# A bidirectional encoder block on one core: two feature tiles side by side in the opening

## The chip, the cores and the metric

One core of one Trainium2 chip runs the whole program. The metric is the device time of one execution in microseconds (us), measured as the median of several runs; lower is better. The core has TensorE (matrix products, "PE" in the profile, with "PEld" for its weight loads), VectorE ("DVE"), ScalarE ("ACT"), GpSimd ("POOL"), and SyncE ("SP"), whose queue issues nearly all transfers here.

## The reference

Two groups of tokens, a prompt of 2048 and a sample of 512, go through one layer of a hybrid encoder with shared weights. Sixteen learned meta tokens stand ahead of each.

```python
u = rms_norm(h, norm_g)
proj = u @ w_in                      # 1024 -> 5376, cut into ten parts
qa, ka, va, za, qb, kb, vb, zb, ga, gb = jnp.split(proj, cuts, axis=-1)
o_a = neighbourhood_attention(qa, ka, va, na_rpb, n)     # branch A: 8 x 16 window on a 64-wide grid
o_b = window_attention(qb, kb, vb, t5_bias, sink, n)     # branch B: +-128 tokens, 8 query and 2 key heads
y_a = (o_a * jax.nn.silu(za)) @ w_proj_a
y_b = (o_b * jax.nn.silu(zb)) @ w_proj_b
merged = jax.nn.sigmoid(ga) * y_a + jax.nn.sigmoid(gb) * y_b
h = h + merged @ w_out
y = rms_norm(h[:, N_META:], final_g)                     # rms_norm: x * rsqrt(mean(x*x) + 1e-6) * g
```

All inputs and outputs are float32.

## The kernel before

Everything is kept feature-major: 128 features on the partitions, tokens along the free dimension. The 2560 tokens are five windows of 512 (window 0 is the sample, 1 to 4 the prompt). The 5376 output features of the input projection are 42 feature tiles of 128: branch A's queries are tiles 0 to 3 (`QA`), its keys 4 to 7 (`KA`), its values 8 to 11 (`VA`), its gate path from 12; branch B's queries are 16 to 19 (`QB`), then `KB`, `VB` and its gate path; the merge gates are 26 to 41.

Products are in float32 precision built of three: every operand is split into a rounded high part and the low remainder (`split`, `split_w`, `split_part`: a cast on ScalarE, then a subtraction on VectorE that needs the cast's result), and `mm3` (L143 to L146) adds high x high, high x low and low x high. One feature tile over 512 tokens is therefore 8 input tiles x 3 = 24 products of 128x512, and `project` yields after each quarter of them, that is after two input tiles or 6 products.

The program begins with the last window, which is done alone (`alone`, `beside`), while the inputs of windows 0 and 1 are prepared beside it; these two are then multiplied together in a scheme with fewer products (`begin`, `pairs`). The opening is made of these parts:

- `start_w(firsts)` fetches and splits the weights of the first feature tiles. Raw weights (`wraw`, 512 KB a tile) and split ones (`wt`) have two buffers each, so a third fetch waits for the first tile's split, and a third split for the end of the first tile's products.
- `prep_last(True)` loads the last window's x in four pairs of tiles (`xt`, 512 KB each) and the 16 meta columns (`xm`), scales them by the norm's gain (`ng`) into the high part (ScalarE, L325) and the low part (VectorE, L326), squares them in place (ScalarE, L328) and adds the squares (VectorE, L330, L333). Its later steps, each ended by a `yield`, form the column sums by products with ones (`fin_v`, L351, L352), take the inverse root (`rsqrt`), put it on a diagonal (`diagonal`, L175) and spread it over the partitions by products with ones (`spread`, L183), which are copied to `rs`. The scale is applied only when a product is stored, so products run ahead of the norm and the stores of the first tiles are held back (`held`) until it is there.
- `prep_first` loads windows 0 and 1 (`x`, eight transfers of 512 KB, in two halves), squares them (L409), adds the squares for one window on GpSimd and for the other on VectorE (L411, L414), then does the same norm and forms the operands.
- `zero_rows` writes zeros into twelve places of the value buffers in HBM; all transfers share the queue of SyncE in program order.
- `beside` goes through `firsts` (branch A's queries, branch B's queries, A's keys, A's values, `KB`, `VB`) tile by tile and counts quarters in `q`. At quarters 9 and 14 it takes the two later steps of `prep_last`, at quarters 2, 20, 27, 28 and so on those of `prep_first`. With tile i it fetches the weights of tile i + 3 and splits the next one's.

`store` puts a finished tile away: `put_q` scales it (L272), splits it (L244, L245) and writes it to HBM; a query tile of branch A is written twice over (1 MB), one of branch B once (512 KB).

TensorE's and SyncE's orders are those of the program (`manual_schedule`). On ScalarE, VectorE and GpSimd a planner sets the order, from its own timeline and the program order; `issue_after` adds an edge to it.

After the opening come the pairs of windows 0 and 1, the same for 2 and 3 (with `prep_ahead` beside the first), then attention and the dense layers window by window, and the last window's end.

Of the kernel before, what the change touches and what calls it, by code (L numbers as in the profile page):

```python
# [17 lines left out]
P = 128  # L18
# [77 lines left out]
def encoder_block(ctx: ExitStack, tc: tile.TileContext, xT, x_end, w_in, w_pa, w_pb, w_o, norm_g, final_g,  # L96
# [42 lines left out]
    def move(out, in_):  # L139
        last_move[0] = nc.sync.dma_start(*(f32(a) if a.dtype == F32R else a for a in (out, in_)))  # L140
        return last_move[0]
# [3 lines left out]
        nc.tensor.matmul(ps, wh, ul, start=False, stop=False)  # L145
        nc.tensor.matmul(ps, wl, uh, start=False, stop=last)  # L146

    def rsqrt(small, sq, m, nc_):

        ve, hv, r, t = (small.tile([P, 8], F32, tag=f"rs{i}", name=f"rs{i}")[:m, :nc_] for i in range(4))  # L150
        nc.vector.tensor_scalar(ve, sq, 1.0 / D_MODEL, EPS, ALU.mult, ALU.add)
        nc.vector.tensor_scalar(r.bitcast(I32), ve.bitcast(I32), 1, None, ALU.arith_shift_right)
        nc.vector.tensor_scalar(r.bitcast(I32), r.bitcast(I32), -1.0, float(0x5F3759DF), ALU.mult, ALU.add)
        nc.vector.tensor_scalar(hv, ve, -0.5, None, ALU.mult)
        for _ in range(3):
            if nc_ == 1:
                nc.vector.scalar_tensor_tensor(t, r, hv, r, ALU.mult, ALU.mult)
            else:
                nc.vector.tensor_mul(t, r, hv)
                nc.vector.tensor_mul(t, t, r)  # L160
            nc.vector.scalar_tensor_tensor(r, t, 1.5, r, ALU.add, ALU.mult)
        return r
# [34 lines left out]
    def split_part(h, l, r, eng=None):  # L197
        nc.scalar.copy(h, r)  # L198
        low[0] = (eng or lo_eng[0]).tensor_sub(l, r, f32(h)).ins  # L199
# [8 lines left out]
    class Weights:  # L208
# [50 lines left out]
    def finish(gen):  # L259
        r = None  # L260
        for r in gen:
            pass
        return r
# [41 lines left out]

        return (up if i < 5 else uxp).tile(shape, F32R, tag=f"u{i}", name=name)

    def prep_last(meta):


        w = NWIN - 1
        uh, ul = (operand(i, [P, KT, PITCH], f"u4{i}") for i in (5, 6))
        us[w] = (uh, ul, us[w][2] if w in us else uxp.tile([P, UW + N_META], F32, tag="rs4", name="rs4")[:, :UW])
        rs = us[w][2]
        for k in range(0, KT, 2):
            rows = xT[k * P : (k + 2) * P]
            xt = ev.tile([P, 2, WTOK], F32, tag="ev", name="xt")
            move(xt, rows[:, w * WTOK : (w + 1) * WTOK].rearrange("(k p) t -> p k t", p=P))
            if meta and k == 0:
                xm = st.tile([P, KT, N_META], F32, tag="xm", name="xm", bufs=1)  # L320
                move(xm, xT[:, TOK:].rearrange("(k p) t -> p k t", p=P))
            for j in range(2):
                g = ng[:, k + j : k + j + 1]
                h = uh[:, k + j, :WTOK]
                nc.scalar.mul(h, xt[:, j, :], g)  # L325
                nc.vector.scalar_tensor_tensor(ul[:, k + j, :WTOK], xt[:, j, :], g, f32(h), ALU.mult, ALU.subtract)  # L326
            if meta:
                nc.scalar.activation(xt, xt, AF.Square)  # L328
                if k == 0:
                    nc.vector.tensor_add(rs[:, :WTOK], xt[:, 0, :], xt[:, 1, :])  # L330
                else:
                    for j in range(2):
                        nc.vector.tensor_add(rs[:, :WTOK], rs[:, :WTOK], xt[:, j, :])  # L333
        if not meta:
            return
        t = ev.tile([P, WTOK], F32, tag="t", name="xms", bufs=3)
        a, b = (t[:, i * P : (i + 1) * P].rearrange("p (k m) -> p k m", m=N_META) for i in range(2))
        nc.vector.tensor_mul(a, xm, ng[:, :, None].broadcast_to([P, KT, N_META]))
        mh, ml = uh[:, :, WTOK:UW], ul[:, :, WTOK:UW]
        nc.scalar.copy(mh, a)  # L340
        nc.vector.tensor_sub(ml, a, f32(mh))
        nc.scalar.activation(b, xm, AF.Square)
        for n in (4, 2):
            nc.vector.tensor_add(b[:, :n], b[:, :n], b[:, n : 2 * n])
        nc.vector.tensor_add(rs[:, WTOK:], b[:, 0], b[:, 1])
        yield
        sq = st.tile([P, 32], F32, tag="sq", name="sq", bufs=1)[:, :5]
        nc.vector.memset(sq, 1.0)
        v = ps_t.tile([P, WTOK], F32, tag="vt", name="fin_v")
        for c in range(4):  # L350
            nc.tensor.matmul(v[:, c : c + 1], rs[:, c * P : (c + 1) * P], ones[:, 0:1], start=True, stop=True)  # L351
        nc.tensor.matmul(v[:N_META, 4:5], rs[:, WTOK:], ones[:, 0:1], start=True, stop=True)  # L352
        nc.scalar.copy(sq[:, :4], v[:, :4])
        nc.scalar.copy(sq[:N_META, 4:5], v[:N_META, 4:5])
        r = rsqrt(uxp, sq, P, 5)
        dgs = [ev.tile([P, WTOK], F32, tag="t", name="rs_dg", bufs=3) for _ in range(2)]
        diagonal(dgs[0], r[:, :4], P)
        diagonal(dgs[1], r[:N_META, 4:5], N_META)
        yield
        for dg, c0, m, nc_ in (dgs[0], 0, P, 4), (dgs[1], WTOK, N_META, 1):  # L360
            nc.scalar.copy(rs[:, c0 : c0 + nc_ * m], spread(ps_t, "vt", dg, m, nc_)[:, : nc_ * m])
        yield
# [25 lines left out]
    def prep_first(sp, wa, loaded):  # L388
# [28 lines left out]
        for i in range(2):  # L417
            for c in range(4):
                nc.tensor.matmul(v[:, 4 * i + c : 4 * i + c + 1], rss[i][:, c * P : (c + 1) * P], ones[:, 0:1],
                                 start=True, stop=True)  # L420
        r = rsqrt(uxp, v[:, :8], P, 8)
        dgs = [ev.tile([P, WTOK], F32, tag="t", name="rs_dg", bufs=3) for _ in range(2)]
        for i in range(2):
            diagonal(dgs[i], r[:, 4 * i : 4 * i + 4], P)
# [32 lines left out]
    def prep_ahead(w):  # L457
# [21 lines left out]
        r = rsqrt(uxp, v[:, :8], P, 8)  # L479
# [429 lines left out]
    def beside(fs, raws, wts, own, wa, steps, at):  # L909

        held = [own, None if own is None else []]
        ws = [*fs, *both[0]]
        lag[0] = 4
        mark[0] = None
        at = list(at)
        q = 0
        for i, f in enumerate(fs):
            if i:  # L920
                wts.append(split_w(raws[i + 1]))
                if i + 3 < len(ws):
                    raws.append(fetch_w(w_in[ws[i + 3]]))
            for _ in alone(f, wts[i], held):
                q += 1
                if own is not None and q in own[1]:
                    next(own[0])
                    if q == own[1][-1]:
                        for fn in held[1]:
                            fn()  # L930
                        held[1] = None
                while at and at[0] <= q:
                    at.pop(0)
                    next(steps)
# [13 lines left out]
    order = [*range(0, KA + 2), VA, VA + 1, KA + 2, KA + 3, QB, QB + 1, VA + 2, VA + 3, QB + 2, QB + 3, KB, VB,  # L948
             *range(ZA, QB), *range(ZB, 42)]
    both = list(zip(order[::2], order[1::2]))  # L950
    firsts = [*range(QA, KA), *range(QB, KB), *range(KA, ZA), KB, VB]
    rest = [f for f in range(GA) if f not in firsts]

    def start_w(fs):
        raws = [fetch_w(w_in[f]) for f in fs[:1]]
        wts = [split_w(raws[0])]
        yield raws, wts
        raws.append(fetch_w(w_in[fs[1]]))
        raws.append(fetch_w(w_in[fs[2]]))
        yield  # L960
        wts.append(split_w(raws[1]))
        raws.append(fetch_w(w_in[fs[3]]))
        yield
# [3 lines left out]
            pool = [pp.enter_context(tc.tile_pool(name=f"p{i}", bufs=1, reuse_waits="tile")) for i in range(3)]  # L967
            return pairs(pool, wa, wa + 1, both, a, first.send(pool[2]), raw1, ahead, extra, opening)

    w0 = start_w(firsts)  # L970
    raws, wts = next(w0)
    own = prep_last(True)
    next(own)
    with tc.tile_pool(name="sp", bufs=1, reuse_waits="tile") as sp:
        loaded = []
        steps = prep_first(sp, 0, loaded)
        next(w0)
        next(steps)
# [677 lines left out]
```

## Time and profile before

| | us |
|---|---|
| median of 3 runs | 1897.26 |
| lowest and highest | 1896.54, 1899.39 |
| the profiled execution | 1896.82 |
| its span, first to last instruction | 1894.7 |
| TensorE busy in it | 1863.0 |

A row of the timeline reads: start, duration, engine, source line, operation, tile written <- tiles read, shapes, count, and in brackets the idle time of the engine before it with what ended that. "SPq" rows are transfers being issued, not transferred. A row of the windows reads: stretch, its length, then busy time and count for TensorE, its weight loads, VectorE, ScalarE and GpSimd, the granted clock, the mean busy share of the DMA engines, and GB/s. In a row of the waits, the engine, tile and line on the left waited for what stands on the right: microseconds in total, times, longest.

### The profile page before, as it was taken

Reading aid. Unit: us, or ns where it says so; the run is one execution under the profiler, and the core shown is the slowest. Engines: PE = TensorE matmul, PEld = TensorE weight load, DVE = VectorE, ACT = ScalarE, POOL = GpSimd, SP = SyncE. Lnnn points to the kernel's source line nnn. Section 1 sums busy time; section 2 is a strip of 40 time slices with the busy share of each in tenths; the row PEclk is TensorE's granted clock in tenths of the full one; section 3 lists DMA queues with packets and bytes.
Section 4 is the critical chain, followed back from the end, with each engine's and each line's share of the span. In section 5 each row is a group of like instructions: output and inputs, shape, how many; then the busy total and the mean of one; then the engine's idle time right before and its main releaser. Section 6 shows DMA issues by size and latency. Waiting matters only on the chain. (4 is left out here: it accounts for less than half of the span.)

```text
span 1894.7 us, 29723 instructions
## 1 busy us (share of the span) xinstructions
PE 1863.0 (98%) x9797; PEld 1585.1 (84%) x9797; DVE 1341.5 (71%) x2939; ACT 1144.3 (60%) x2523; POOL 733.1 (39%) x556
## 2 busy tenths in 40 slices
PE   8999999999999999999999999999999999999998
PEld 6898888888888888888888888888888888888886
DVE  8886666556477565444457888878888887888874
ACT  6454444444365444444456787897788778778932
POOL 2005442323102232323224336656754864585420
PEclk9999999999999999999999999999999999999999
DMA  7667756644296787644268878967976996697483
GB/s 262 236 177 293 209 173 183 212 172 178 84 354 227 218 222 199 201 135 160 106 218 306 264 230 264 305 201 254 314 246 216 290 313 212 213 315 253 125 289 141
DMA packets 290385, 424.83 MB, mean 224 GB/s; under 512 B 117416, under 2 KB 162040, under 8 KB 288696
## 3 DMA queue, kind: packets, MB, share of 16 engines
q1 hardware_dynamic: 289944, 422.93, 69.2%
q8 instruction: 78, 1.28, 0.3%
q14 instruction: 75, 0.61, 0.1%
q10 hardware_dynamic: 288, 0.01, 0.0%
HBM read 303.46 MB, written 119.39 MB: 223 GB/s over the span
## 5 line engine op out<-in xcount | busy, mean ns | idle before, releaser
L199 POOL TENSOR_TENSOR wt<-wraw,wt 128x512 fp32r<-128x512 f32 x164 | 215.0, 1328 | 283.9 <-ACT wt L198 283.9
L826 PE MATMUL pa<-u,wt 128*128 128x512 f32 x1008 | 242.7, 390 | 0.0
L826 PE MATMUL pa<-u,x 128*128 128x512 f32 x984 | 236.8, 389 | 0.9 <-ACT u L837 0.9
L198 ACT CAST wt<-wraw 128x512 fp32r<-128x512 f32 x312 | 177.7, 619 | 77.0 <-PE mm L146 36.4
L826 PEld LDWEIGHTS pa<-u,wt 128*128 128x128 f32 x1008 | 188.8, 188 | 39.1
L826 PEld LDWEIGHTS pa<-u,x 128*128 128x128 f32 x984 | 184.4, 188 | 40.1 <-ACT u L837 1.7
L797 POOL TENSOR_TENSOR s<-wraw,raw 128x512 f32<-128x512 f32 x40 | 58.3, 1457 | 275.1 <-DVE x L199 275.1
L144 PE MATMUL mm<-u,wt 128*128 128x512 f32 (+2 forms) x416 | 150.8, 362 | 8.0 <-ACT u L325 7.4
L792 POOL TENSOR_TENSOR s<-raw 128x512 f32<-128x512 f32 x40 | 58.4, 1461 | 253.5 <-DMA raw<-in_w_in_dram 250.1
L146 PE MATMUL mm<-u,wt 128*128 128x512 f32 (+2 forms) x416 | 147.1, 354 | 1.9 <-DVE wt L199 1.9
L145 PE MATMUL mm<-u,wt 128*128 128x512 f32 (+2 forms) x416 | 147.0, 353 | 0.7 <-DVE u L326 0.7
L199 DVE TENSOR_TENSOR wt<-wraw,wt 128x512 fp32r<-128x512 f32 x148 | 107.9, 767 | 53.2 <-ACT wt L198 52.8
L826 PE MATMUL pe<-u,wt 128*128 128x512 f32 x504 | 121.3, 390 | 0.0
L826 PE MATMUL pc<-u,wt 128*128 128x512 f32 x504 | 121.1, 389 | 0.0
L826 PE MATMUL pe<-u,x 128*128 128x512 f32 x480 | 115.3, 389 | 0.0
L826 PEld LDWEIGHTS pc<-u,wt 128*128 128x128 f32 x504 | 94.6, 188 | 19.6
L826 PEld LDWEIGHTS pe<-u,wt 128*128 128x128 f32 x504 | 94.5, 188 | 19.6
L1122 DVE TENSOR_TENSOR pl<-tp,ph 128x384 fp32r<-128x384 f32 (+6 forms) x160 | 94.5, 591 | 22.3 <-ACT ph L1121 20.6
L144 PE MATMUL pso<-mh,wt 128*128 128x512 f32 x256 | 107.1, 418 | 0.0
L805 POOL TENSOR_TENSOR s<-wraw,s 128x512 f32<-128x512 f32 x40 | 55.0, 1374 | 131.5 <-DVE wt L199 131.5
L826 PEld LDWEIGHTS pe<-u,x 128*128 128x128 f32 x480 | 90.1, 188 | 18.7
L1027 ACT ACTIVATE prs<-s,nm 128x402 f32<-128x402 f32 (+1 forms) x160 | 91.0, 571 | 20.8 <-DVE nm L1020 17.7
(246 smaller groups left out, 5028.0 us busy)
## 6 DMA issues: line engine op xcount, KB each, us to landing
wraw<-in_w_in_dram SPq DMA_DIRECT2D x86, 512.0 KB
qa<-evq SPq DMA_DIRECT2D x20, 1024.0 KB
raw<-in_w_in_dram SPq DMA_DIRECT2D x40, 512.0 KB
q<-qa SPq DMA_DIRECT2D x20, 1024.0 KB
wraw<-in_w_o_dram SPq DMA_DIRECT2D x32, 512.0 KB
kbt<-kb SPq DMA_DIRECT2D x32, 384.0 KB
qb<-evq SPq DMA_DIRECT2D x20, 512.0 KB
ka<-evk SPq DMA_DIRECT2D x20, 512.0 KB
```

Of the source, the lines that this page charges most:

```text
L144: nc.tensor.matmul(ps, wh, uh, start=first, stop=False)
L145: nc.tensor.matmul(ps, wh, ul, start=False, stop=False)
L146: nc.tensor.matmul(ps, wl, uh, start=False, stop=last)
L198: nc.scalar.copy(h, r)
L199: low[0] = (eng or lo_eng[0]).tensor_sub(l, r, f32(h)).ins
L792: eng.tensor_add(s1, a21, a22)
L797: eng.tensor_sub(s3, a11, a21)
L805: eng.tensor_sub(s4, a12, s2)
L826: nc.tensor.matmul(ps, wt[:, a, s], u[:, b, kk, :], start=first and kk == 0 and i == 0, stop=kk == 3 and i == 2, skip_group_check=True)
L1027: nc.scalar.activation(out, s, AF.Exp, bias=nm, scale=-1.0, accum_out=sm)
L1122: nc.vector.tensor_sub(pl_[:kb, a], tb, f32(ph_[:kb, a]))
```

## The change

The opening is rewritten in these points.

1. The first two feature tiles are done side by side. `start_two` fetches their weights by halves (256 KB each) and splits each half by itself; `prep_last` takes it as a generator `between` and moves it on between the x loads and between the scalings, so that transfers are issued as: first tile's lower half, x tile 0, x tile 1, second tile's lower half, x tiles 2 and 3, both upper halves, the other x tiles. In `beside`, `first_two` alternates the quarters of the two tiles 0, 1, 0, 1, 0, 0, 1, 1.
2. The meta columns are loaded behind all x of the window.
3. Nine products of ones with ones, 128x128, go to TensorE ahead of everything. Nothing reads their result.
4. The squares of `prep_last` are placed behind all scalings, in a step of their own; `issue_after` holds them there on ScalarE.
5. `firsts` begins with branch B's queries, then branch A's.
6. The steps beside the tiles move: `prep_last`'s from quarters 9 and 14 to 10 and 15, `prep_first`'s second from 20 to 22.
7. In `rsqrt`, the half term is computed from the sums and not from the step before it, and in the input norms the root `r` lives in columns 8 to 15 of the accumulator bank that holds the sums (`place`); `prep_last`'s two copies of the sums are gone.

```diff
-    def rsqrt(small, sq, m, nc_):
+    def rsqrt(small, sq, m, nc_, place=None):
         ve, hv, r, t = (small.tile([P, 8], F32, tag=f"rs{i}", name=f"rs{i}")[:m, :nc_] for i in range(4))
+        if place is not None:
+            r = place[:m, :nc_]
...
-        nc.vector.tensor_scalar(hv, ve, -0.5, None, ALU.mult)
+        nc.vector.tensor_scalar(hv, sq, -0.5 / D_MODEL, -0.5 * EPS, ALU.mult, ALU.add)
...
-    def prep_last(meta):
+    def prep_last(meta, between=None):
...
+        xts = []
         for k in range(0, KT, 2):
             xt = ev.tile([P, 2, WTOK], F32, tag="ev", name="xt")
-            move(xt, rows[:, w * WTOK : (w + 1) * WTOK].rearrange("(k p) t -> p k t", p=P))
-            if meta and k == 0:
-                xm = st.tile([P, KT, N_META], F32, tag="xm", name="xm", bufs=1)
-                move(xm, xT[:, TOK:].rearrange("(k p) t -> p k t", p=P))
+            xts.append(xt)
+            for j, n in ((0, 1), (1, 1)) if meta and k == 0 else ((0, 2),):
+                move(xt[:, j : j + n], xT[(k + j) * P : (k + j + n) * P, w * WTOK : (w + 1) * WTOK]
+                     .rearrange("(k p) t -> p k t", p=P))
+            if between is not None:
+                next(between, None)
             for j in range(2):
...
-                nc.scalar.mul(h, xt[:, j, :], g)
+                scaled = nc.scalar.mul(h, xt[:, j, :], g)
                 nc.vector.scalar_tensor_tensor(ul[:, k + j, :WTOK], xt[:, j, :], g, f32(h), ALU.mult, ALU.subtract)
-            if meta:
-                nc.scalar.activation(xt, xt, AF.Square)
...
+            if between is not None:
+                next(between, None)
         if not meta:
             return
+        xm = st.tile([P, KT, N_META], F32, tag="xm", name="xm", bufs=1)
+        move(xm, xT[:, TOK:].rearrange("(k p) t -> p k t", p=P))
+        yield
+        for k, xt in enumerate(xts):
+            with tc.issue_after(scaled.ins):
+                nc.scalar.activation(xt, xt, AF.Square)
+            if k == 0:
+                nc.vector.tensor_add(rs[:, :WTOK], xt[:, 0, :], xt[:, 1, :])
+            else:
+                for j in range(2):
+                    nc.vector.tensor_add(rs[:, :WTOK], rs[:, :WTOK], xt[:, j, :])
...
-        sq = st.tile([P, 32], F32, tag="sq", name="sq", bufs=1)[:, :5]
-        nc.vector.memset(sq, 1.0)
         v = ps_t.tile([P, WTOK], F32, tag="vt", name="fin_v")
+        nc.vector.memset(v[:, 4:5], 1.0)
...
-        nc.scalar.copy(sq[:, :4], v[:, :4])
-        nc.scalar.copy(sq[:N_META, 4:5], v[:N_META, 4:5])
-        r = rsqrt(uxp, sq, P, 5)
+        r = rsqrt(uxp, v[:, :5], P, 5, v[:, 8:16])
...
-        r = rsqrt(uxp, v[:, :8], P, 8)
+        r = rsqrt(uxp, v[:, :8], P, 8, v[:, 8:16])
...
+        def first_two():
+            gens = [alone(fs[i], wts[i], held) for i in range(2)]
+            for i in (0, 1, 0, 1, 0, 0, 1, 1):
+                next(gens[i])
+                yield
+            for g in gens:
+                finish(g)
...
-            for _ in alone(f, wts[i], held):
+            if own is not None and i < 2:
+                quarters = first_two() if i == 0 else ()
+            else:
+                quarters = alone(f, wts[i], held)
+            for _ in quarters:
...
-    firsts = [*range(QA, KA), *range(QB, KB), *range(KA, ZA), KB, VB]
+    firsts = [*range(QB, KB), *range(QA, KA), *range(KA, ZA), KB, VB]
...
-    w0 = start_w(firsts)
-    raws, wts = next(w0)
-    own = prep_last(True)
+    def start_two(raws, wts):
+        for f in firsts[:2]:
+            raws.append(wpool.tile([P, KT * P], F32, tag="wraw", name="wraw"))
+            wts.append(wpool.tile([P, 2, KT * P], F32R, tag="wt", name="wt"))
+        def fetch(i, c):
+            move(raws[i][:, c], w_in[firsts[i]][:, c])
+        def part_of(i, c):
+            split_part(wts[i][:, 0, c], wts[i][:, 1, c], raws[i][:, c])
+        fetch(0, lo)
+        part_of(0, lo)
+        yield
+        fetch(1, lo)
+        yield
+        part_of(1, lo)
+        yield
+        fetch(0, hi)
+        fetch(1, hi)
+        yield
+        part_of(0, hi)
+        part_of(1, hi)
+        yield
+    warm_up = ps_t.tile([P, WTOK], F32, tag="vt", name="warm")
+    for _ in range(9):
+        nc.tensor.matmul(warm_up[:, :P], ones, ones, start=True, stop=True)
+    raws, wts = [], []
+    w0 = start_two(raws, wts)
+    next(w0)
+    own = prep_last(True, w0)
     next(own)
     with tc.tile_pool(name="sp", bufs=1, reuse_waits="tile") as sp:
         loaded = []
         steps = prep_first(sp, 0, loaded)
-        next(w0)
+        raws.append(fetch_w(w_in[firsts[2]]))
         next(steps)
-        next(w0)
+        next(own)
+        raws.append(fetch_w(w_in[firsts[3]]))
         loaded.append(last_move[0])
         next(steps)
         zero_rows()
-        begun = beside(firsts, raws, wts, (own, (9, 14)), 0, steps, [2, 20, 27, *(28 + 27 * i // 10 for i in range(16))])
+        begun = beside(firsts, raws, wts, (own, (10, 15)), 0, steps,
+                       [2, 22, 27, *(28 + 27 * i // 10 for i in range(16))])
```

More of the change, by code (lines that the diff above doesn't have):

```diff
@@ L314, in prep_last @@
         rs = us[w][2]
+        xts = []
         for k in range(0, KT, 2):
-            rows = xT[k * P : (k + 2) * P]
             xt = ev.tile([P, 2, WTOK], F32, tag="ev", name="xt")
-            move(xt, rows[:, w * WTOK : (w + 1) * WTOK].rearrange("(k p) t -> p k t", p=P))
-            if meta and k == 0:
-                xm = st.tile([P, KT, N_META], F32, tag="xm", name="xm", bufs=1)
-                move(xm, xT[:, TOK:].rearrange("(k p) t -> p k t", p=P))
+            xts.append(xt)
[4 more added lines that the diff above has]
+                next(between, None)
             for j in range(2):
@@ L324, in prep_last @@
                 h = uh[:, k + j, :WTOK]
-                nc.scalar.mul(h, xt[:, j, :], g)
+                scaled = nc.scalar.mul(h, xt[:, j, :], g)
                 nc.vector.scalar_tensor_tensor(ul[:, k + j, :WTOK], xt[:, j, :], g, f32(h), ALU.mult, ALU.subtract)
-            if meta:
[L328 to L333, printed above, removed]
+            if between is not None:
+                next(between, None)
         if not meta:
             return
+        xm = st.tile([P, KT, N_META], F32, tag="xm", name="xm", bufs=1)
[9 more added lines that the diff above has]
+                    nc.vector.tensor_add(rs[:, :WTOK], rs[:, :WTOK], xt[:, j, :])
         t = ev.tile([P, WTOK], F32, tag="t", name="xms", bufs=3)
@@ L478, in prep_ahead @@
                                  start=True, stop=True)
-        r = rsqrt(uxp, v[:, :8], P, 8)
+        r = rsqrt(uxp, v[:, :8], P, 8, v[:, 8:16])
         dgs = [ev.tile([P, WTOK], F32, tag="t", name="rs_dg", bufs=3) for _ in range(2)]
```

## The prediction

> **What bounds the kernel now.** I read the page first, then TensorE's waits, then the timeline of the first 60 us by engine, then the traffic by windows. The page says how much there is to win at all:
>
> ```profile
> span 1894.7 us, 29723 instructions
> PE 1863.0 (98%) x9797; PEld 1585.1 (84%) x9797; DVE 1341.5 (71%) x2939; ACT 1144.3 (60%) x2523; POOL 733.1 (39%) x556
> ```
>
> TensorE is idle for 1894.7 - 1863.0 = 31.7 us. Its order is written by hand, so the end comes earlier only by idle time or slow products taken away. The waits view of TensorE up to 640 us has four lines (who, for whom: total, times, longest):
>
> ```profile
> PE mm L144 <- ACT u L325: 7.4, 1, 7.4
> PE mm L146 <- DVE wt L199: 1.9, 1, 1.9
> PE rs_rb L183 <- DVE rs_dg L175: 1.1, 1, 1.1
> PE mm L144 <- ACT wt L198: 0.6, 1, 0.6
> ```
>
> They sum to 11.0 us, all of it before 60 us, which is just the stretch that the change rewrites. The timeline of TensorE shows where they lie (start, duration, engine, line):
>
> ```profile
> 7.42 0.79 PE L144 MATMUL mm<-u,wt 128*128 128x512 f32 x1 [7.42 <-ACT u L325]
> ...
> 14.01 0.40 PE L144 MATMUL mm<-u,wt 128*128 128x512 f32 x1
> ...
> 22.65 0.39 PE L146 MATMUL mm<-u,wt 128*128 128x512 f32 x1
> 22.88 0.95 PE L351 MATMUL fin_v<-ones,rs 128*128 128x1 f32 x8
> ...
> 32.04 1.48 PE L183 MATMUL rs_rb<-rs_dg,ones 128*128 128x128 f32 x10 [1.06 <-DVE rs_dg L175]
> ...
> 36.80 0.47 PE L146 MATMUL mm<-u,wt 128*128 128x512 f32 x1
> ...
> 57.21 0.50 PE L144 MATMUL mm<-u,wt 128*128 128x512 f32 x1 [0.60 <-ACT wt L198]
> 59.81 0.50 PE L146 MATMUL mm<-u,wt 128*128 128x512 f32 x1 [1.87 <-DVE wt L199]
> ```
>
> From 14.01 to 22.65 there are 38 steps: 0.227 us a product. The product at 14.01 is the sixteenth, so the first fifteen took (14.01 - 7.42)/15 = 0.44 us each. The profile's granted clock is 1.00 in all windows of this stretch (the column after the counts in the rows below), so the slow pace is read from the starts alone. The 48 products of two feature tiles are through at 14.01 + 33 x 0.227 = 21.5 us; at full pace they need 10.9.
>
> What supplies them, from the timelines of ScalarE, VectorE, GpSimd and the queue:
>
> ```profile
> 4.52 1.14 ACT L198 CAST wt<-wraw 128x512 fp32r<-128x512 f32 x2 [1.85 <-DMA wraw<-in_w_in_dram]
> 6.65 1.33 ACT L325 ACTIVATE u<-xt,ng 128x512 fp32r<-128x512 f32 x2 [0.99 <-DMA xt<-in_xT_dram]
> 9.51 1.04 ACT L328 ACTIVATE xt<-xt 128x1024 f32<-128x1024 f32 x1
> 7.40 1.41 DVE L326 SCALAR_TENSOR_TENSOR u<-xt,ng,u 128x512 fp32r<-128x512 f32 x2
> 24.74 0.16 DVE L151 TENSOR_SCALAR rs<-sq 128x5 f32<-128x5 f32 x1
> 26.15 1.19 DVE L160 TENSOR_TENSOR rs<-rs,rs 128x5 f32<-128x5 f32 x1
> 30.21 1.86 DVE L175 TENSOR_TENSOR rs_dg<-ident,rs 128x512 f32<-128x512 f32 x2
> 33.18 2.94 DVE L414 TENSOR_TENSOR rsp<-rsp,sq 128x512 f32<-128x512 f32 x4 [0.51 <-DVE rsp L411]
> 36.04 1.28 DVE L199 TENSOR_TENSOR wt<-wraw,wt 128x512 fp32r<-128x512 f32 x2
> 26.02 5.42 POOL L414 TENSOR_TENSOR rsp<-rsp,sq 128x512 f32<-128x512 f32 x4 [2.36 <-ACT sq L409]
> 0.74 0.39 SPq L140 DMA_DIRECT2D wraw<-in_w_in_dram  x1
> 29.32 8.36 SPq L140 DMA_DIRECT2D wraw<-in_w_in_dram  x3
> 42.16 4.20 SPq L140 DMA_DIRECT2D qa<-evq  x4
> 46.45 1.33 SPq L140 DMA_DIRECT2D wraw<-in_w_in_dram  x1
> ```
>
> and the traffic by stretches (last two columns: mean busy share of the DMA engines, GB/s):
>
> ```profile
> 5.25:6.25 1.00, 0.00 (x0) 0.00 (x0) 1.00 (x2) 0.41 (x1) 0.00 (x0) 1.00 1.35 210
> 6.25:25.50 19.25, 18.08 (x71) 14.47 (x72) 18.47 (x33) 15.22 (x25) 4.54 (x3) 1.00 1.03 377
> 25.50:31.00 5.50, 5.49 (x25) 4.21 (x23) 5.12 (x10) 4.28 (x5) 4.75 (x4) 1.00 0.61 141
> 31.00:32.50 1.50, 0.46 (x4) 0.46 (x5) 1.50 (x3) 0.00 (x0) 0.44 (x1) 1.00 0.85 325
> ```
>
> Up to 25.5 us the loads are one unbroken stream at 377 GB/s (0.69 us for 256 KB, 1.38 for 512 KB). Then come the zero rows, small writes at 141 GB/s, and behind them, issued from 29.32, the fifth tile's weights.
>
> **The change part by part.** *Halves and the order of loads.* The first transfer is half as long, so the first cast (4.52) comes 0.69 earlier, at 3.8, and 256 KB of x follow at 4.5. The meta columns, now in the stream at 5.25 to 6.25 (210 instead of 377 GB/s, 0.4 to 1 us lost), go behind the last x. The first scaling also needs the gain vector. No row shows its landing; it is there by 6.65. Between 4.5 and 6.65 I take 4.8, near the first, because it is 4 KB and issued ahead of everything. From scaling to product it is 7.42 - 6.65 = 0.77: first product at 5.6. If the vector is the late one, it stays at 7.4.
>
> *Two tiles side by side.* Behind the first half come three more of 256 KB, 512, two of 256 and two of 512: 3.8 + 5 x 0.69 + 3 x 1.38 = 11.4 for the last x. Two scalings (1.33) end at 12.7, VectorE's last (0.71) at 13.4. A pair of x tiles feeds twelve products (2.7 us) instead of six, so demand and supply are even: without loss of pace the 48 are through at about 16.9, held by data at the start only.
>
> *The nine products ahead.* They need nothing that is loaded, so they start at about 1, and write a bank that nobody reads. The five such products from 32.04 (x10 rows) take 1.41 us to the next product, 0.28 each; nine are 2.5 us at full pace and 4.9 at the slow one (0.44/0.227). They are over by 3.5 to 5.9, a delay of 0.3 to the first product at the worst. They are worth what they bring the change of pace forward. Bounds: all (16.9) or nothing (fifteen products that lose 0.21 each, 3.2 on 5.6 + 10.9: 19.7). If time since the first product counts, 6.6 us from 1, the pace changes at 7.6 and the end is 17.6. I take 17.9. The Trainium skill, "TensorE: Matmul & The Clock Gate", section "What's actually happening", says that a gate halves the clock until a free-running window of about 3.4 us has been busy. By it a window that holds the pause between the nine and the first real product doesn't count, and unless the phase is lucky the end is nearer 19.7.
>
> *Squares behind the scalings, chain in the accumulator bank.* Four squares (1.04 each) leave the scalings' way and run from 12.7 to 16.9 on ScalarE. Seven additions of 0.7 and the meta column's small work put the sums at about 20 to 21; the products on them come after ten quarters now, at 17.9 + 2 x 1.36 = 20.6. The chain from 24.74 to 30.21 + 1.86 = 32.07 lasts 7.3 us: thirteen steps on VectorE, of which one like 26.15 takes 1.19 instead of 0.16 while GpSimd adds from 26.02. Two copies go, and with r in the accumulator bank I take 0.2 a step and 0.65 a diagonal: 4 us, inside the five quarters (6.8 us) that it has. If the stretching stays it is 7.3 again and TensorE waits 0.5. The Trainium skill, "SBUF — State Buffer", "SBUF: two separate sides", speaks for the 4 us: VectorE is locked out by GpSimd only with two SBUF inputs or in a two-port mode.
>
> So TensorE could reach the fifth tile at 17.9 + 8 x 1.36 + 1.0 + 1.4 = 31.2 instead of 36.35 (36.80 less two steps). **But the fifth tile's weights are not there.** The stream carries the same bytes up to the zero rows, and gets a hole: the third weights wait on the queue for the first weights' buffer, whose upper half is split by about 10.1, and all eight x loads stand behind them. A load into an empty stream took 3.8 us from issue (0.74) to cast (4.52), so these land at 13.9; unbroken they would land at 11.4 + 0.6 + 1.38 = 13.4. Hole: 0.5. The zero rows and their cost on the queue are as before. The fifth weights, now in at about 33 (traffic back from 31.0, 512 KB at 325 GB/s is 1.6, some 0.4 to the semaphore), come at 33.5; cast 0.57, subtraction 0.64, hand-overs 0.3: third product of the fifth tile at 35.0 instead of 36.80. **First term: 1.8 us**, whatever was won ahead of it. Bounds: 0, if VectorE does the sums first as from 33.18 on (the split at 36.04 follows on them), and 5.5 if the weights are no limit and the start is fast.
>
> *Branch B's queries first.* What is late at 57 to 60 is the eighth tile's weights, issued at 46.45 behind four query stores. Sizes from the page:
>
> ```profile
> qa<-evq SPq DMA_DIRECT2D x20, 1024.0 KB
> qb<-evq SPq DMA_DIRECT2D x20, 512.0 KB
> ```
>
> Four of 1 MB take 11 us of stream, four of 512 KB 5.5. The eighth weights then land at about 48 to 51 and are wanted at 54. A's stores come later, one a tile: 1 MB and 512 KB of weights are 4.1 us of stream in a tile's 5.4, hidden; without that cover they bring back the wait they caused. **Second term:** 0.60 + 1.87 = **2.5 us.**
>
> *Second norm.* Its sums are wanted at about 43 and VectorE, which had them at 37 to 41, has more room. Its chain gets five quarters (6.8 us) instead of seven for some 5 us: hidden, up to 1 us if VectorE is behind. The later norms lie where TensorE does not wait for them: nothing.
>
> Sum: 1.8 + 2.5 = 4.3 us. This execution took 1896.82 us (span 1894.7 and 2.1 around it): 1892.5. The median of the runs, 1897.26, is 0.4 above it; I say **1892.6**.
>
> **The rivals.** *A, the weights do not bind* (0.26): the zero rows' place is not set by their bytes (141 GB/s); if they go sooner, the first term is 36.35 - 31.2 = 5.1, from 3.3 with the slow start (19.7) to 5.5: 5.8 to 8.0 won, 1888.8 to 1891.0. Against: they stand behind a stream that was full anyway. The clock rule decides only between these two ends.
>
> *B, VectorE is the limit* (0.13): 33.18 to 36.04 shows sums ahead of the split, and the three held stores now fall in the same microseconds. Then the first term is nil and the second loses up to 1 us: 1894.3 to 1895.3.
>
> *C, no effect* (0.04): the shorter second chain gives back the rest too, 1896.8.
>
> *D, slower* (0.07): the order on ScalarE, VectorE and GpSimd is a planner's and is made anew. Between 640 and 1850 us TensorE is idle for 1210.0 - 1197.6 = 12.4 us:
>
> ```profile
> 640.00:1850.00 1210.00, 1197.63 (x6605) 1025.35 (x6603) 890.75 (x2196) 827.23 (x1959) 570.97 (x435) 1.00 0.74 234
> ```
>
> If GpSimd and VectorE meet there more often and this doubles, 12.4 - 4.3 = 8.1 us are lost: 1904.9. It decides from a growth by two thirds (8.1 us, 3.8 more than is won). Against: past 60 us the hand-written order stands as it was, only earlier.
>
> **How the numbers follow.** The forecast has 0.50, with 2.8 to 5.8 us won, 1891.0 to 1894.0. 0.2% is 3.8 us, about what a measurement of this kernel can tell from no change; three quarters of the forecast lie beyond it. Faster 0.26 + 0.38 = 0.64; within 0.12 + 0.13 + 0.04 + 0.01 of D = 0.30; slower 0.06. The range goes from A's best with 0.8 of scatter, 1888.0, to B's worst with 0.9, 1896.2; D, most of C and the tails stay out.
>
> **What would show it.** First product before 6 us; 48 of them through by 19.7; no gap ahead of the first spreading products; TensorE waiting for the split at the fifth tile, at 34 to 35; no wait at the eighth; the chain's steps on VectorE all near 0.2. I am wrong if the fifth tile starts by 32 (A), if its third product is at 36.8 again (B), or if the idle time past 640 us grows (D).

## The result: 15.4 us slower

The median of the changed kernel is 1914.56 us (5 runs, 1910.91 to 1915.20), that of the kernel before beside it 1898.54 us; the ratio is 1.0081, with a 95% interval from 1.0068 to 1.0094. That is 15.4 us by the ratio and 16.0 by the medians. The forecast was 1892.6 us. The profiled execution, the fastest of the five, took 1910.91 us:

```profile
span 1908.8 us, 29764 instructions
PE 1879.8 (98%) x9815; PEld 1590.0 (83%) x9815; DVE 1338.6 (70%) x2939; ACT 1145.4 (60%) x2521; POOL 736.0 (39%) x556
```

The span is 14.1 us longer, but TensorE is idle for only 1908.8 - 1879.8 = 29.0 us, 2.7 less than before. The loss is busy time: TensorE has 16.8 us more of it. The 18 additional entries are the nine products ahead (4.2 us, first row below); the other 12.6 us must be products that are slower than they were. So waits alone are not the loss.

The opening did much of what was forecast (timeline of TensorE after: start, duration, engine, line, operation):

```profile
1.06 4.21 PE L1021 MATMUL warm<-ones 128*128 128x128 f32 x18 [1.06 <-DVE ones L126]
5.68 0.50 PE L144 MATMUL mm<-u,wt 128*128 128x512 f32 x1 [0.41 <-ACT u L331]
...
18.35 0.39 PE L146 MATMUL mm<-u,wt 128*128 128x512 f32 x1
...
30.81 1.37 PE L186 MATMUL rs_rb<-rs_dg,ones 128*128 128x128 f32 x10
...
35.69 0.63 PE L144 MATMUL mm<-u,wt 128*128 128x512 f32 x1 [1.91 <-ACT wt L201]
36.12 0.63 PE L145 MATMUL mm<-u,wt 128*128 128x512 f32 x1
36.89 0.79 PE L146 MATMUL mm<-u,wt 128*128 128x512 f32 x1
...
57.70 0.39 PE L144 MATMUL mm<-u,wt 128*128 128x512 f32 x1
```

The first product starts at 5.68 instead of 7.42, the 48th at 18.35 instead of 21.29, the spreading products no longer wait, and at 57.70 no wait stands ahead of the eighth tile. What is new is the wait of 1.91 us at the fifth tile and the slow products behind it. ScalarE, VectorE and the queue show why (their timelines after):

```profile
35.02 1.14 ACT L201 CAST wt<-wraw 128x512 fp32r<-128x512 f32 x2 [1.51 <-DMA wraw<-in_w_in_dram]
...
26.00 0.15 DVE L155 TENSOR_SCALAR fin_v<-rs 128x5 int32<-128x5 int32 x1
...
28.18 0.17 DVE L164 SCALAR_TENSOR_TENSOR fin_v<-rs,fin_v 128x5 f32<-128x5 f32 x1
28.45 0.76 DVE L178 TENSOR_TENSOR rs_dg<-ident,fin_v 128x512 f32<-128x512 f32 x2
...
11.57 0.34 SPq L140 DMA_DIRECT2D wraw<-in_w_in_dram  x1
...
31.17 7.22 SPq L140 DMA_DIRECT2D wraw<-in_w_in_dram  x3
```

The fifth weights go on the queue at 31.17, 1.85 us later than before (29.32), and ScalarE stands idle for 1.51 us until they land. The slow products are a halved clock (windows of after, cut where the granted clock changes; it is the column behind the five engines):

```profile
32.51:35.92 3.41, 1.50 (x7) 0.93 (x6) 3.41 (x5) 1.90 (x4) 0.78 (x1) 1.00 0.84 298
35.92:39.33 3.41, 3.26 (x8) 2.04 (x8) 3.41 (x7) 2.94 (x6) 0.00 (x0) 0.50 0.14 19
39.33:42.75 3.42, 3.42 (x17) 2.79 (x16) 3.42 (x6) 0.00 (x0) 0.00 (x0) 1.00 0.86 332
```

The waits of TensorE up to 640 us name a second place that was not there before (who, for whom: total, times, longest):

```profile
PE pa L835 <- ACT wt L201: 3.1, 1, 3.1
PE mm L144 <- ACT wt L201: 2.1, 2, 1.9
PE pa L835 <- DVE wt L202: 1.8, 1, 1.8
```

`pa` is a product of the pairs, so this lies at the seam where `beside` ends and `begin` takes over. ScalarE and TensorE there, after:

```profile
127.00 0.62 ACT L201 CAST wt<-s 128x512 fp32r<-128x512 f32 x1 [2.94 <-DVE s L801]
127.53 0.58 ACT L846 COPY s<-pa 128x512 f32<-128x512 f32 x1
128.00 4.26 ACT L381 CAST u<-x 128x512 fp32r<-128x512 f32 x8
132.16 0.61 ACT L201 CAST wt<-s 128x512 fp32r<-128x512 f32 x1
...
132.83 0.73 PE L835 MATMUL pa<-u,wt 128*128 128x512 f32 x2 [3.08 <-ACT wt L201]
135.39 3.91 PE L835 MATMUL pa<-u,wt 128*128 128x512 f32 x10 [1.82 <-DVE wt L202]
```

and ScalarE before:

```profile
127.28 0.62 ACT L198 CAST wt<-s 128x512 fp32r<-128x512 f32 x1 [3.90 <-DVE s L792]
128.43 0.62 ACT L198 CAST wt<-s 128x512 fp32r<-128x512 f32 x1 [0.53 <-DVE s L793]
128.95 0.58 ACT L837 COPY s<-pa 128x512 f32<-128x512 f32 x1
129.43 4.27 ACT L372 CAST u<-x 128x512 fp32r<-128x512 f32 x8
```

The eight casts of the last operands (4.26 us), which nobody awaits so soon, stood behind the two casts of the pair's weights; now they stand between them, and the second half of the weights, which TensorE needs next, comes at 132.77 instead of 129.05.

Behind the seam no wait is left up to 640 us, and still TensorE does less (windows of before, then of after; the first pair of numbers behind the length is TensorE's busy time and its count):

```profile
140.00:640.00 500.00, 500.00 (x2231) 414.44 (x2230) 307.71 (x444) 232.83 (x408) 151.66 (x108) 1.00 0.62 210
```

```profile
140.00:640.00 500.00, 500.00 (x2205) 409.99 (x2205) 297.99 (x438) 231.03 (x405) 150.61 (x106) 1.00 0.61 207
640.00:1850.00 1210.00, 1199.53 (x6593) 1024.10 (x6592) 892.43 (x2191) 829.37 (x1962) 573.90 (x437) 1.00 0.73 230
```

Twenty-six products fewer in 500 us, busy throughout in both kernels and at a granted clock of 1.00. Two groups of the page, before and then after (out<-moving operand, weights; count; busy time, mean ns of one), show which products are slow:

```profile
L826 PE MATMUL pa<-u,x 128*128 128x512 f32 x984 | 236.8, 389 | 0.9 <-ACT u L837 0.9
L826 PE MATMUL pe<-u,x 128*128 128x512 f32 x480 | 115.3, 389 | 0.0
```

```profile
L835 PE MATMUL pa<-u,x 128*128 128x512 f32 x984 | 242.6, 395 | 0.7 <-ACT u L846 0.7
L835 PE MATMUL pe<-u,x 128*128 128x512 f32 x480 | 118.4, 396 | 0.0
```

The same 1464 products with weights in the tiles `x` take 8.9 us more, 6 ns each. From start to start it is the same: 226.8 ns before, 232.8 and 233.2 after (means over these groups between 100 and 1000 us).

To place all this, the table counts the projection and dense products of TensorE (tiles `mm` and `p...`; the first is number 0) and gives the start of the n-th in a run minus its start in the run of before, in us. Each column is one profiled execution. The columns to the right are experiments that follow.

| product (start before) | after | a_pad | a_seam | w_qbfirst | a_zero | a_zero2 |
|---|---|---|---|---|---|---|
| 47 (21.3) | -2.9 | -2.5 | -3.2 | 0.0 | -2.7 | -3.4 |
| 98 (36.8) | +0.1 | -0.2 | -0.2 | -0.1 | -2.7 | -3.1 |
| 143 (49.0) | +1.3 | +1.5 | -0.2 | -0.1 | +4.4 | -5.0 |
| 191 (64.7) | -1.8 | -1.6 | -3.2 | -3.1 | +1.8 | -6.2 |
| 680 (127.7) | -1.8 | -1.6 | -3.2 | -3.1 | +1.8 | -6.2 |
| 800 (155.5) | +5.3 | +5.9 | -2.8 | +2.9 | +2.3 | -6.2 |
| 3000 (659.9) | +11.8 | +5.9 | -2.9 | +3.7 | +2.3 | -6.2 |
| 4700 (1082.3) | +15.7 | +8.6 | -1.3 | +3.7 | +3.1 | -4.1 |

So the opening gives 1.8 us, the seam takes some 7, and from there to product 3000 another 6.5 are lost, which `a_pad` does not lose. Behind product 3000 both lose: after 3.9 us more, `a_pad` 2.7.

### The profile page after: what moved, and what is told of

Read it like the earlier page. It is cut to its first block, busy times and chain, and to the rows that moved or that the text cites. A ratio compares the mean times of both kernels' runs of the same rounds, so it can differ in the third digit from the quotient of the medians.

```text
span 1908.8 us, 29764 instructions
## 1 busy us (share of the span) xinstructions
PE 1879.8 (98%) x9815; PEld 1590.0 (83%) x9815; DVE 1338.6 (70%) x2939; ACT 1145.4 (60%) x2521; POOL 736.0 (39%) x556
## 4 chain that ended last, share of the span: by engine, by line
PE 76%; DVE 9%; ACT 6%; DMA 4%; issue 2%; POOL 2%; SPq 0%; DVEq 0%; ACTq 0%; POOLq 0%
PE pa L835 24%; PE pe L835 12%; PE pc L835 6%; PE mm L146 3%; PE mm L145 3%; PE mm L144 3%; PE pso L146 2%; PE pso L144 2%; PE pso L145 2%; PE tp L1173 2%; DVE s L1075 1%; DVE pr L1093 1%; PE tp L1275 1%; DVE pl L1283 1%; PE oa L1190 1%
## 5 line engine op out<-in xcount | busy, mean ns | idle before, releaser
L835 PE MATMUL pa<-u,x 128*128 128x512 f32 x984 | 242.6, 395 | 0.7 <-ACT u L846 0.7
```

What stands on the lines that cost most here:

```text
L835: nc.tensor.matmul(ps, wt[:, a, s], u[:, b, kk, :], start=first and kk == 0 and i == 0, stop=kk == 3 and i == 2, skip_group_check=True)
```

## The experiments

**The slow products: addresses.** The change drops the 128-byte tile `sq` from the pool `st`. Everything allocated behind it moves down by 128 bytes: the weight tiles `x` of the pairs from 480 to 352 (addresses modulo 512, as the programs are laid out), while the operands `u` stay at 224. Theory: the placing of these weights costs 6 ns a product. Rival: the products are slow because other engines or transfers, differently timed, disturb TensorE. `a_pad` is the changed kernel with an unused tile of 128 bytes in the old place; the order on every engine is unchanged.

```diff
+        st.tile([P, 32], F32, tag="pad", name="pad", bufs=1)
         v = ps_t.tile([P, WTOK], F32, tag="vt", name="fin_v")
```

> The changed kernel with one unused tile of 128 bytes a partition where the removed tile of the sums stood, so that the pools behind it lie at their old addresses; the order of every engine is the same. Theory 'address': the products whose weights come from those pools go back from about 233 to 227 ns a step, and the execution loses 10 to 12 us, to 1899 to 1904. Rival 'something else slows the products' (clock, traffic, order): no change, 1911 to 1915.

Measured: 1906.32 us, ratio to before 1.0043 (1.0030 to 1.0055), 8.2 us under the changed kernel (7.2 by the two ratios). My range, 1899 to 1904, was missed, but not by this group, which is back:

```profile
L836 PE MATMUL pa<-u,x 128*128 128x512 f32 x984 | 236.8, 389 | 2.2 <-ACT u L847 2.2
```

The reverse test puts 128 bytes more into the kernel before, at the same place (`b_pad128`):

> The kernel before with one unused tile of 128 bytes more at that place, all orders the same. Theory 'address': the products with weights from the moved pools (pa and pe from x) slow from 227 to about 233 ns, and the execution is some 10 to 12 us longer, 1907 to 1911. If only the sum of the change's edits slows them: no change, 1896 to 1900.

Measured, one run: 1906.23 us, just under my range, with the slow group (page of b_pad128):

```profile
L827 PE MATMUL pa<-u,x 128*128 128x512 f32 x984 | 242.5, 395 | 0.0
```

The shift alone, with the order on every engine unchanged, makes and unmakes the slow products; the rival is out. What about the address counts? `b_const128` puts the 128 bytes at the start of the first pool instead, so that `wt`, `u0` to `u4` and `x` all move (to 352, 352 and 96), but `u5` and `u6` stay at 224:

> The kernel before with 128 bytes more at the very start of the memory, so that the weights' buffers, five of the seven operands and the moved pools all shift together and keep their distance; the last two operands and their neighbours lie at the other side and stay. Theory 'absolute address': all products of the projection slow by some 6 ns, more than twice the loss of the shifted pools alone, 25 us or more. Theory 'distance between weights and operand': only products of moved weights with the two operands that stay are slow, or none; under 8 us.

Measured, one run: 1906.69 us, and not one answer for a group but two (page of b_const128):

```profile
L827 PE MATMUL pa<-u,x 128*128 128x512 f32 x984 | 239.5, 392 | 0.0
L827 PE MATMUL pe<-u,x 128*128 128x512 f32 x480 | 118.5, 395 | 0.0
```

`pe<-u,x` multiplies by `u6` only (96 against 224: 128 apart), and is slow. `pa<-u,x` holds products with `u4` (96 against 352: 256 apart) and with `u5` (128 apart), and lies half-way. The trace tells the two apart by what stands ahead of them: the twelve behind `pe<-u,wt` (`u4`) take 226.8 ns from start to start, the twelve behind `pc<-u,wt` (`u5`) 232.6. So no address by itself is good or bad; the distance between weights and moving operand counts. My size, under 8 us, was missed: the products of single tiles (`mm`, weights at 352, operand at 224) became slow too, 233.1 ns from start to start, which I had not counted. Two more shifts at the place of `b_pad128` test the period:

```diff
+        st.tile([P, 16], F32, tag="pad", name="pad", bufs=1)   # b_pad64; b_pad256 has [P, 64]
```

> The kernel before with 64 unused bytes where the change takes 128 out. If only a distance of 128 modulo 256 between weights and moving operand is slow, the products over x stay at 226.8 ns and the time within 3 us of before. If every distance that isn't a multiple of 256 is slow, they take about 230 to 233 ns and the time is 5 to 11 us above before.

> As b_pad64 with 256 bytes. If the rule is a distance modulo 256, the products over x stay at 226.8 ns and the time within 3 us of before. If any move of these tiles costs (another neighbour, another bank), 232 to 233 ns and 8 to 11 us more.

Measured, one run each: 1907.33 us with 64 bytes, 1896.32 us with 256. The group in b_pad64:

```profile
L827 PE MATMUL pa<-u,x 128*128 128x512 f32 x984 | 243.0, 396 | 0.0
```

and in b_pad256:

```profile
L827 PE MATMUL pa<-u,x 128*128 128x512 f32 x984 | 237.0, 390 | 0.8 <-ACT u L838 0.8
```

Of the distances tried, 0 and 256 modulo 512 are fast and 64, 128 are slow: a distance that is a multiple of 256 bytes is what the kernel before had, and the change took it away.

**The seam.** Theory: the planner's place for the second cast costs what the table shows between products 680 and 800. Rival: the wait there is only an echo of the later opening or of the clock. `a_seam` is `a_pad` with the last steps (and their eight casts) held behind both casts of the pair's weights; the orders of ScalarE and VectorE differ there only.

```diff
-        first = sides_first(raws[-2:], wts[-1])
+        first, casts = sides_first(raws[-2:], wts[-1]), high[-2:]
...
-        with tc.issue_after(copied[0]):
+        with tc.issue_after(copied[0]), tc.issue_after(casts[0]), tc.issue_after(casts[1]):
```

> The changed kernel with the 128 bytes put back and, at the seam to the pairs, an edge that keeps the eight casts of the last operands behind both casts of the first pair's weights. Theory 'seam': TensorE's waits of 3.1 and 1.8 us there go, with the slow pace that follows, 5 to 7 us less than with the 128 bytes alone, 1894 to 1897. Rival 'the casts wait for late weights anyway': no gain over the 128 bytes alone.

Measured: 1896.75 us, ratio to before 0.9999 (0.9990 to 1.0008), 9.6 us under `a_pad`; by the table 8.7 at product 800, of which 1.6 were there at 680. The 1.6 come from the opening, where the clock was halved in `a_pad` (37.58 to 40.99 us) and not in `a_seam`; they are not the edge's doing. The seam's own 7.1 are just over my 5 to 7. Behind the two waits (3.0 and 1.5 us in `a_pad`) the clock was halved too (a window of a_pad):

```profile
136.00:139.00 3.00, 3.00 (x8) 2.31 (x7) 1.82 (x4) 0.00 (x0) 0.00 (x0) 0.50 0.63 240
```

The rival is out: an edge at the seam alone takes the waits there away. With both causes undone, the changed kernel is level with the kernel before.

Which part of the change moved the cast? `w_qbfirst` is the kernel before with the order of the two branches' queries alone exchanged:

```diff
-    firsts = [*range(QA, KA), *range(QB, KB), *range(KA, ZA), KB, VB]
+    firsts = [*range(QB, KB), *range(QA, KA), *range(KA, ZA), KB, VB]
```

> The kernel before with the order of the two branches' queries alone exchanged; no tile is dropped, so the addresses stay. In the order that is built, the second cast of the pair's weights stands behind the eight operand casts at the seam again, as in the changed kernel. If that order costs what a_seam took back (7 to 9 us by product 800), less the 2.5 us of the eighth tile, the median is 4.5 to 6.5 us above before: 1902 to 1904, with the products over x at 226.8 ns. If the wait at the seam only arose together with the changed opening, it is 2 us below before: 1895.

Measured: 1900.17 us, ratio 1.0014 (1.0005 to 1.0023). The waits at the seam are there in full (TensorE's waits, w_qbfirst):

```profile
PE pa L826 <- ACT wt L198: 2.6, 1, 2.6
PE pa L826 <- DVE wt L199: 1.2, 1, 1.2
```

The exchange by itself is enough to move the cast. It gives 3.1 us at the eighth tile and loses 6.0 at the seam (table). I had expected a loss of 4.5 to 6.5 us and got 2.8: the seam cost at least 1 us less than I took, and the eighth tile gave 0.6 us more.

**The opening.** `a_qafirst` is `a_seam` with branch A's queries first again:

> a_seam with branch A's queries first again, everything else as there (the casts at the seam stay held by the edges). If the second term is right, the eighth tile's weights come behind the four larger qa stores again and TensorE waits 2 to 2.5 us near 57 to 60 us: median 1898.7 to 1899.3. If the fifth tile's wait has already moved everything enough, no wait there and 1896.7.

Measured: 1896.85 us, ratio 0.9995 (0.9986 to 1.0005), and no wait at the eighth tile; product 680 stands at -3.5 us. The theory's number was wrong, the rival's right. The queue of a_qafirst shows how:

```profile
39.31 4.95 SPq L140 DMA_DIRECT2D qa<-evq  x4
44.35 1.33 SPq L140 DMA_DIRECT2D wraw<-in_w_in_dram  x1
```

With the changed opening the four large stores go at 39.31 instead of 42.16, and the weights behind them at 44.35 instead of 46.45. The eighth tile's wait is removed once by the opening and once by the exchange; it can be won only once.

`a_nowarm` is `a_seam` without the nine products ahead:

> a_seam without the nine products ahead of the opening. The first real products then run at half pace for 3.4 us, which puts the 47th product about 1.7 us later than in a_seam. If the fifth tile's weights bound the opening (first term of the prediction), the 98th product and everything from 191 on come within 0.4 us of a_seam: median 1896.5 to 1897.2. If the opening is bound by TensorE's own work, 1.7 us stays to the end: 1898.4.

Measured: 1896.75 us, ratio 0.9996 (0.9987 to 1.0005), the median of `a_seam` to the digit. In its profiled execution the 47th product is 1.4 us later than in `a_seam`, the 98th 0.7, and product 680 is 3.2 later, since a half-clock stretch follows the fifth tile's wait here and does not in `a_seam`'s. The medians say that the nine products win nothing that can be measured; the one profile does not fit my 0.4 us, and with a single profile each the 3.2 stay open.

`a_zero` takes away what the fifth weights wait for: the zero rows go behind the sixth weights.

```diff
-        zero_rows()
         begun = beside(...)
...
+            if own is not None and i == 2:
+                zero_rows()
```

> a_seam with the twelve zero-row stores issued behind the sixth tile's weights instead of ahead of the fifth's. If the weights that queue behind the zero rows hold TensorE at the fifth tile (96th to 98th product), both waits there go (1.1 and 1.2 us in a_seam), the 98th product comes 2 to 4 us earlier than in a_seam, and of that at least 2 us is left at product 680: median 1892.5 to 1894.7. If VectorE's order (low parts, evictions) is what binds next, the waits only move to a wt or a bank of another tile: under 1 us, 1896 to 1897.

Measured: 1900.08 us, ratio 1.0011 (1.0002 to 1.0019): slower than `a_seam`. The fifth tile's wait did go (98th product -2.7 us), but TensorE now waits longest elsewhere (waits of a_zero):

```profile
PE fin_v L429 <- DVE rsp L424: 2.9, 1, 2.9
```

The planner put the earlier weights' low parts, and stores of the first tiles, ahead of additions of the second norm's squares on VectorE, and the column sums, at a fixed place among TensorE's products, came before those were done. The clock was halved behind this wait as well (a window of a_zero):

```profile
46.00:49.00 3.00, 3.00 (x14) 2.94 (x14) 0.44 (x3) 0.00 (x0) 0.00 (x0) 0.50 0.92 240
```

Together that cost 7 us (table, 98 to 143). Two versions move the sums and what follows by some quarters:

```diff
-                       [2, 22, 27, *(28 + 27 * i // 10 for i in range(16))])
+                       [2, 25, 29, *(30 + 26 * i // 10 for i in range(16))])   # a_zero2
+                       [2, 24, 29, *(29 + 27 * i // 10 for i in range(16))])   # a_zero3
```

> a_zero with the second prep's sums moved from the 22nd quarter of a tile's products to the 25th, their spread from the 27th to the 29th and the scalings two later. If a_zero lost its gain only because TensorE stood 2.9 us at those sums while VectorE still added the squares, the wait goes and the 2.4 us by which the 98th product came ahead of a_seam stay to product 680: 5 to 6 us ahead of before there, median 1892.5 to 1895. If VectorE itself is the limit of the opening, the wait reappears at the following spread, at an operand or at a bank: 1896 or more.

> As a_zero2 with the sums at the 24th quarter and the scalings one later instead of two. If 2.9 us of wait are covered by two quarters of 1.36 us, a wait of under 0.5 us is left at the sums and the time is that of a_zero2 within 1 us. If VectorE is the limit, it waits there for more.

Measured: `a_zero2` 1895.17 us, ratio 0.9982 (0.9973 to 0.9991); `a_zero3` 1894.06 us, ratio 0.9982 (0.9973 to 0.9992). The sums no longer wait (TensorE, a_zero2: no bracket behind the row):

```profile
45.54 1.84 PE L429 MATMUL fin_v<-ones,rsp 128*128 128x1 f32 x16
```

In `a_zero3` they do not wait either, but the clock was halved behind them (47.09 to 50.50 us), and product 680 is 4.4 us ahead. The two medians are 1.1 us apart, where I had said within 1.

These two beat both kernels: 3.4 us (0.18%) under before by the ratio, 2.5 and 3.6 by the medians, some 19 under the changed kernel. `a_zero2` is 6.2 us ahead at product 680, a little over what I expected, and ends 4.1 ahead at product 4700. Every version of the changed kernel falls back between products 3000 and 4700, those with the addresses put right by 0.3 (`a_qafirst`) to 2.7 us (`a_pad`); none of the runs tells where it comes from.

## Why the prediction was wrong

*The start* was right: first product at 5.6 (5.68), 48 products through by 17.9 (18.35), the chain's steps near 0.2 us (0.15 to 0.17), no gap ahead of the spreading products. The size of the 18.35 is in part luck: the clock rose at 5.20 us in this execution and at 10.27 in that of `a_pad`, which has the same orders and comes to 18.81. The granted clock of 1.00 that the prediction read for the slow first products of before is no reading: the first clock record of that trace is the change to the full clock at 13.61 us, and the view shows 1.00 where there is none.

*The first term, 1.8 us*, had the right mechanism and the wrong size. The fifth tile waited for weights behind the zero rows, but its third product came at 36.89, not at 35.0. The step that failed is "Hole: 0.5": VectorE split the first tile's upper half only from 10.86 on, and the third weights went on the queue at 11.57, not near 10.1. The stream of loads broke off for longer (a window of after; the last column is GB/s):

```profile
11.00:13.60 2.60, 2.60 (x13) 2.15 (x12) 2.51 (x5) 2.23 (x5) 0.00 (x0) 1.00 0.78 139
```

Against 377 GB/s that is 2.60 x (1 - 139/377) = 1.6 us of stream lost, not 0.5. All x loads of windows 0 and 1 and the zero rows stand behind it, so that the fifth weights were issued 1.85 us later than before, not at the same time. What I did not have at all is the price of the wait itself: half clock for 3.4 us behind it, so that +0.1 at the 98th product became +1.3 (table). `a_zero` shows that the weights were the limit, and that VectorE, rival B, is the next one; in `a_zero2`, with both out of the way, the opening gives 6.2 us, near the best of rival A (5.8 to 8.0).

*The second term, 2.5 us*, is right as a size: 3.1 from the 143rd to the 191st product in the changed kernel and 3.1 alone in `w_qbfirst`. But it is not a term to be added: `a_qafirst` has it without the exchange.

*"Past 60 us the hand-written order stands as it was, only earlier"* is the step that failed with the largest consequence I could have seen. The order of TensorE is written by hand; that of ScalarE at the seam is the planner's, and the exchange of the queries changed it there. Rival D had the mechanism in the wrong place: between 640 and 1850 us the idle time fell from 12.4 to 1210.0 - 1199.53 = 10.5 us, and the harm was done in 8 us around 130. It cost 9.6 us by medians (1906.32 to 1896.75) and 7.1 in the traces of `a_pad` and `a_seam` between products 680 and 800, the half clock behind the waits included.

*The dropped tile* was costed at nothing, without a sentence. The sum takes it that every product past the opening keeps its pace; 128 bytes less made those over `x` 6 ns slower each. It cost 8.2 us by medians (1914.56 to 1906.32). In the traces, from product 800 to 4700, `b_pad128` falls back by 9.4 us and after by 10.4, of which `a_pad` loses 2.7 without it.

Together: 8.2 and 9.6 us lost against `a_seam`, and an opening that is worth 3 us in the traces up to product 680 and less than the measurement can tell at the end (1896.75 against 1897.50).

## What to carry to other kernels

When an edit adds or drops a tile, compare the addresses of the tiles behind it, and keep the distance between weights and moving operand of the hot products where it was measured to be fast, here a multiple of 256 bytes (a pad of 128 bytes put it back). When an order is made by a planner, compare the orders of all engines before and after over the whole program, not only where the edit is, and hold the few places that matter by explicit edges. A wait of 2 us on TensorE can cost another 1 to 2 us by the clock behind it (1.2 in after and 1.7 in `a_pad` from the 98th to the 143rd product), so the granted clock is to be read there before a wait is priced.

## What the runs showed of the hardware

- A 128x512 product takes 226.8 ns from start to start when weights and moving operand lie a multiple of 256 bytes apart, and 232.6 to 233.3 ns at the other distances tried (64 and 128 modulo 256). No address by itself was slow (`b_const128`). The slow pace lasts a little into the next group: in after, the group `pa<-u,wt`, whose tiles did not move, went from 226.9 to 228.5 ns, but its first eight products behind `pa<-u,x` and `pe<-u,x` take 230.5 and 228.1 ns and the last four 226.7 and 226.8. What in the chip makes the distance count, no run here shows.
- Ahead of the program's last microseconds, TensorE's clock was halved in stretches of 3.41 us, or two or three of them in a row, and within a trace all changes of the clock lie on one grid of that step: in after it falls at 35.92, rises at 39.33, falls at 134.90 and rises at 138.32, and 134.90 - 39.33 = 95.57 is 28 x 3.413. Where an execution's work falls on this grid differs (full clock from 5.20 in after, from 10.27 in `a_pad`). In the window of the grid ahead of the first fall TensorE was busy for 1.50 of 3.41 us. In `a_seam`, with two waits of 1.1 and 1.2 us, it was busy for 1.87 there, and the clock stayed at 1.00 (a_seam):

```profile
32.48:35.89 3.41, 1.87 (x7) 0.86 (x6) 3.41 (x6) 2.55 (x6) 0.53 (x1) 1.00 0.50 201
35.89:39.31 3.42, 2.71 (x12) 2.25 (x13) 3.42 (x7) 2.17 (x5) 0.00 (x0) 1.00 0.18 29
```

The Trainium skill, "TensorE: Matmul & The Clock Gate", section "What's actually happening", has the clock halved after an idle free-running window of about 3.4 us. The grid and its step agree with that; that the window must be idle does not, since TensorE was busy for 44% of the window ahead of the slow one. The busy time does not settle it either: 1.58 us in before (57.98 to 61.39) kept the full clock, 1.71 in `a_pad` (34.16 to 37.58) lost it, and so did 3.31 in `a_zero3` (43.68 to 47.09), where 1.9 us of the busy time are the sixteen products of 128x1. What the gate counts, the runs do not tell.
